# A decoder layer on one core: the weight sums of the MLP's product 5 in the tiles of product 7, and two tiles in place of three for the down projection's operands

## The chip, the cores and the metric

The kernel runs on one NeuronCore of one Trainium2 chip. The metric is the device time of one execution in microseconds (us); the kernel before took 1101.72 us, the median of 3 runs (1101.19 to 1101.97).

## What is computed

The reference is one decoder layer on 512 tokens of width 1024, in float32: a retention branch and a latent attention branch, an output projection, an MLP and a gated embedding. The change touches only the MLP, which comes near the end:

```python
h2 = rms_norm(x, norm_mlp)
x = x + jnp.square(jax.nn.relu(h2 @ w_up)) @ w_down     # w_up 1024x4096, w_down 4096x1024
gate = jax.nn.sigmoid(rms_norm(x, norm_ple) @ w_ple_gate)
x = x + gate * (p_l @ w_ple)
```

## The kernel before

All matrix products are made with float32r operands that are split in two: a high part (ScalarE, ACT in the profile, by a copy) and a low part (VectorE, DVE, by a subtraction), and three matmuls in place of one (`mm3`). Weights pass through the same split: `load_chunk` (line 247) makes `wh_...` on ACT and then `wl_...` on DVE from a raw tile of 128x1024 floats, 512 KB.

The MLP's hidden width of 4096 is worked in four groups (`gg` 0 to 3). The up product of group 0 is a plain product of eight chunks (`up`, line 973; chunks `wr_up_0_0` to `wr_up_0_7`, here "up chunk 0" to "up chunk 7"). All other products, the up products of groups 1 to 3 (`up_seven`, line 1024, called u1 to u7) and the down products of all groups (`down`, line 1084, called dn1 to dn7), are made by a scheme with seven half-size products in place of eight, in the order 1, 7, 2, 6, 5, 4, 3. Each product needs two weight chunks (`c` 0 and 1), which are quarters of the weight or sums of them:

- products 1, 2 and 3 use a quarter as it is: one load by the SyncE queue (SP);
- product 7 is loaded by SP and then gets a second quarter added by a DMA that accumulates, which GpSimd (POOL) issues; products 6 and 4 add one more quarter each to the same tile, so that this tile lives from product 7 to product 4;
- product 5 is loaded by SP and gets one quarter added by a DMA of POOL.

`prepare` (line 218) issues these. Raw tiles come from two sets: `wraw`, six tiles in the pool `wpool`, named `wr_...`, for everything that is loaded as it is and, in the MLP, also for product 5; and `draw`, four tiles in the pool `tw` that is opened for the tail, named `dr_...`, for product 7. SP issues its loads in order; a load into a tile waits until the DVE has made the low part of the chunk that was there before. The tile framework's scheduler sets the order of instructions on each engine from the tiles that are free, so a number of tiles changes the order.

A line of code (1365) sets how down and up products alternate: `"1 v3 7 u1 2 6 u7 5 4 u6 3 u2 u5 u4"`, where a number is a down product of this group, `u` an up product of the next group and `v3` product 3 of this group's up. The last group runs `"1 v3 7 2 e 6 e 5 4 3"`, where `e` is part of a small other product. The down product's left operand is split by `xsplit` (line 1050) into `ch` and `cl` tiles, 4 KB per partition each; three of each rotate. `combine` (line 1055) makes the operand of the next down product just ahead of the present one.

Before the seven-product scheme can start, the normalised input is read back from DRAM: `up_norm` (line 989) loads `x2n` in two halves of 1 MB (line 992, DMAs on SP) and scales it in eight DVE instructions (line 994); `up_operand` (line 996) makes the operands `xu...` from it. The prediction speaks of the two halves' landing as T0 and T1. `up_out` (line 978) evacuates the plain up product (`f`, lines 984 and 985).

Of the kernel before, what the change touches and what calls it, by code (L numbers as in the profile page):

```python
# [31 lines left out]
F32R = mybir.dt.float32r  # L32
# [19 lines left out]

C_ID, C_MASK, C_IND, C_INVR, C_INVM, C_SGN, C_N = 0, 128, 256, 260, 261, 262, 263

NDYN, NKEEP, NW, NRAW, NDRAW, AHEAD, PREP, EARLY, PAD = 45, 16, 3, 6, 4, 1, 3, 5, 104
GROUPS = DFF // 1024


# [90 lines left out]
def trunk_layer(ctx: ExitStack, tc: tile.TileContext, xT, pT, pos, gains, const, decay, wstream, outT):  # L149
# [61 lines left out]
    def chunk(key):  # L211
        width, o = spec[key][0], offset[key]
        fetched.add(key)
        return wstream[o:o + P * width].rearrange("(p c) -> p c", p=P)
# [3 lines left out]
    def prepare(key):  # L218

        if key[0] == "sw":  # L220
            _, blk, p, c = key

            def more(raw, kb, fb):
                nc.gpsimd.dma_start(raw, chunk(("w", blk, kb, fb, c)), accum_op=ALU.add)  # L224

            if p in (6, 4):
                return more(dw[blk, "t", c], *((0, 0) if p == 6 else (1, 0)))
            kb, fb = {1: (0, 0), 7: (0, 1), 2: (1, 0), 5: (0, 1), 3: (1, 1)}[p]
            nm = f"{blk[0]}{blk[1]}{p}{c}"
            if p == 7 and blk[0] in ("dn", "up"):  # L230
                raw = tail_pool["w"].tile([P, 1024], F32, tag="draw", name="dr_" + nm, bufs=NDRAW)
            else:
                raw = wpool.tile([P, 1024], F32, tag="wraw", name="wr_" + nm, bufs=NRAW)
            nc.sync.dma_start(raw, chunk(("w", blk, kb, fb, c)))
            dw[blk, "t" if p == 7 else p, c] = raw
            if p == 7:
                more(raw, 1, 1)
            elif p == 5:
                more(raw, 0, 0)
            return  # L240
        width = spec[key][0]
        nm = "_".join(str(x) for x in key)
        raw = wpool.tile([P, width], F32, tag="wraw", name="wr_" + nm, padded_shape=[P, 1024], bufs=NRAW)
        tc.keep_in_program_order(nc.sync.dma_start(raw, chunk(key))) if key[0] == "a1" else nc.sync.dma_start(raw, chunk(key))
        dw[key] = raw
# [25 lines left out]
    def run_steps():  # L271
        order = list(dict.fromkeys(k for k, _, _ in steps if k is not None))
        rank = {k: i for i, k in enumerate(order)}
        loaded, prepared = len(wt), len(dw)
        for key, fn, args in steps:
            if key is not None:
                while loaded < min(len(order), rank[key] + 1 + AHEAD):
                    if prepared == loaded:
                        prepare(order[prepared])
                        prepared += 1  # L280
                    load_chunk(order[loaded])
                    loaded += 1
                while prepared < min(len(order), rank[key] + 1 + PREP) and (tail_pool or order[prepared][0] == "sw"):
                    prepare(order[prepared])
                    prepared += 1
                fn(wt[key], *args)
            else:
                fn(*args)
        assert fetched == set(spec), fetched ^ set(spec)
# [12 lines left out]
    def split(src, name, scale=None, hi=None, lo=None, pin=False):  # L302

        hi = T(name + "h", F32R) if hi is None else hi
        lo = T(name + "l", F32R) if lo is None else lo
        if scale is None:
            ACT(hi, src, AF.Copy)
            TT(lo, src, hi.bitcast(F32), op=ALU.subtract)  # L308
        else:
            i = ACT(hi, src, AF.Copy, scale=scale)  # L310
            if pin:
                tc.keep_in_program_order(i)
            STT(lo, src, scale, hi.bitcast(F32), op0=ALU.mult, op1=ALU.subtract)  # L313
        return hi, lo
# [52 lines left out]
    for k in range(8):  # L367
        xs.append(T(f"x{k}"))
        if k < 6:
            prepare(("a1", k))  # L370
        tc.keep_in_program_order(nc.sync.dma_start(xs[k], xT[:, k]))
# [584 lines left out]
    def A(name, shape, tag, bufs, dtype=F32):  # L956
        return tail_pool["a"].tile([P, *shape], dtype, tag=tag, name=name, bufs=bufs)
# [90 lines left out]
            STT(t, t, 0.0, t, op0=ALU.max, op1=ALU.mult)  # L1048

    def xsplit(gg, p, src, scale=None):  # L1050
        hi = A(f"ch{gg}{p}", (4, 256), "ch", 3, F32R)
        lo = A(f"cl{gg}{p}", (4, 256), "cl", 3, F32R)
        X[gg, p] = split(src, None, scale, hi=hi, lo=lo)

    def combine(gg, p):

        f1, f2 = F[gg, 0], F[gg, 1]
        a11, a21, a12, a22 = f1[:, :, 0:256], f1[:, :, 256:512], f2[:, :, 0:256], f2[:, :, 256:512]

        def tmp(nm):  # L1060
            return A(f"{nm}_{gg}", (4, 256), "cs", 2)

        if p == 1:
            xsplit(gg, p, a11, -1.0)
        elif p == 7:
            X["s"] = tmp("s")
            TT(X["s"], a21, a11, op=ALU.subtract)  # L1067
            xsplit(gg, p, X["s"])
        elif p in (6, 3):
            TT(X["s"], a22 if p == 6 else a12, X["s"], op=ALU.subtract)  # L1070
            xsplit(gg, p, X["s"])
        elif p == 2:
            xsplit(gg, p, a12)
        elif p == 5:
            t = tmp("s1")
            TT(t, a21, a22, op=ALU.subtract)
            xsplit(gg, p, t)
        else:
            xsplit(gg, p, a22, -1.0)
# [142 lines left out]
    for h in range(MH):  # L1222
        p, more = h // 2, h + 2 < MH
# [144 lines left out]
    for gg in range(GROUPS):  # L1368
        last, quarter = gg + 1 == GROUPS, 0
        for s_ in "1 v3 7 2 e 6 e 5 4 3".split() if last else seq:  # L1370
# [5 lines left out]
            elif s_[0] in "uv":  # L1376
                g_, p = gg + (s_[0] == "u"), int(s_[1])
# [4 lines left out]
            else:  # L1382
                p = int(s_)
# [74 lines left out]
```

## Time and profile before

| | |
|---|---|
| median of 3 runs | 1101.72 us (1101.19 to 1101.97) |
| the profiled execution | 1101.0 us, its span 1099.2 us |
| PE busy | 1085.2 us, 99% of the span |
| DVE busy | 757.9 us, 69% |
| ACT busy | 565.8 us, 51% |
| POOL busy | 111.1 us, 10% |
| moved by DMA | 195.91 MB |
| plain queue q1 (issued by SP) | 134.90 MB, 35.7% of the 16 DMA engines' time |
| accumulating queue q0 (issued by POOL) | 60.04 MB, 27.3% |

PE is TensorE's matmul row. Times in the views count from the start of the span. In a timeline a row has the start, the duration, the engine, the line, the operation, the tile written and the tiles read; what stands in brackets is the idle time of that engine just before and what ended it. SPq and POOL rows of DMAs are issues, not transfers. The MLP runs from about 711 us (first up chunk) to about 1040 us.

### The profile page before, as it was taken

What the parts mean: (1) busy time and instruction counts of PE and PEld (TensorE: products, weight loads), DVE (VectorE), ACT (ScalarE), POOL (GpSimd) and SP (SyncE); (2) the same over time, 40 slices, a digit from 0 to 9 for tenths busy, and PEclk for the clock granted to TensorE, in tenths of its full rate; (3) what the DMA queues carried; (4) which work ended last, traced back from release to release, by engine and by line L of the source; (5) the groups of instructions that cost most, each with busy time, mean ns of one, the idle gap of its engine ahead of it and who ended that gap; (6) DMA issues with size and microseconds to landing.
All of it is one profiled execution on the core that took longest, in us unless ns stands there. A gap on an engine that the chain in (4) does not pass through costs nothing. (4 is left out here: it accounts for less than half of the span.)

```text
span 1099.2 us, 14887 instructions
## 1 busy us (share of the span) xinstructions
PE 1085.2 (99%) x5569; PEld 923.3 (84%) x5569; DVE 757.9 (69%) x1176; ACT 565.8 (51%) x817; POOL 111.1 (10%) x145
## 2 busy tenths in 40 slices
PE   9999999999999999999999999999999999999998
PEld 7778888888888888888888888887899899898887
DVE  7697677566774655655465467649869769769784
ACT  7647656444466545344554644426645545546541
POOL 0000000000112001122100100011111111201000
PEclk9999999999999999999999999999999999999999
DMA  7232231356778744498864934694998999979511
GB/s 261 71 120 87 72 107 50 133 199 212 206 190 241 193 157 159 121 196 213 204 205 118 286 126 148 199 305 117 229 267 222 229 272 220 238 217 279 154 47 58
DMA packets 64616, 195.91 MB, mean 178 GB/s; under 512 B 7904, under 2 KB 9312, under 8 KB 64160
## 3 DMA queue, kind: packets, MB, share of 16 engines
q1 hardware_dynamic: 46464, 134.90, 35.7%
q0 software_dynamic: 17936, 60.04, 27.3%
q8 instruction: 44, 0.72, 0.3%
q14 instruction: 28, 0.23, 0.1%
q10 hardware_dynamic: 144, 0.03, 0.0%
HBM read 175.80 MB, written 17.04 MB: 175 GB/s over the span
## 5 line engine op out<-in xcount | busy, mean ns | idle before, releaser
L169 PE MATMUL dn<-wl_dn,ch 128*128 128x512 f32 x224 | 87.7, 391 | 1.5 <-DVE wl_dn L266 1.5
L169 PE MATMUL dn<-wh_dn,cl 128*128 128x512 f32 x224 | 87.7, 391 | 1.4 <-DVE cl L308 0.9
L169 PE MATMUL dn<-wh_dn,ch 128*128 128x512 f32 x224 | 87.2, 389 | 0.0
L262 ACT ACTIVATE wh_up<-wr_up 128x1024 fp32r<-128x1024 f32 x32 | 33.9, 1058 | 44.1 <-PE us L169 13.4
L266 DVE TENSOR_TENSOR wl_up<-wr_up,wh_up 128x1024 fp32r<-128x1024 f32 x32 | 39.1, 1221 | 24.4 <-ACT wh_up L262 24.0
L262 ACT ACTIVATE wh_dn<-wr_dn 128x1024 fp32r<-128x1024 f32 x32 | 33.9, 1059 | 34.1 <-PE us L169 16.5
L169 PEld LDWEIGHTS dn<-wh_dn,cl 128*128 128x128 f32 x224 | 42.1, 188 | 10.5 <-DVE cl L308 1.3
L169 PEld LDWEIGHTS dn<-wl_dn,ch 128*128 128x128 f32 x224 | 42.1, 188 | 10.3 <-DVE wl_dn L266 2.3
L169 PEld LDWEIGHTS dn<-wh_dn,ch 128*128 128x128 f32 x224 | 42.1, 188 | 8.8
L266 DVE TENSOR_TENSOR wl_dn<-wr_dn,wh_dn 128x1024 fp32r<-128x1024 f32 x32 | 39.0, 1220 | 10.7 <-ACT wh_dn L262 10.6
L262 ACT ACTIVATE wh_rv<-wr_rv 128x1024 fp32r<-128x1024 f32 x28 | 29.7, 1059 | 30.6 <-issue 9.9
L262 ACT ACTIVATE wh_rg<-wr_rg 128x1024 fp32r<-128x1024 f32 x28 | 29.6, 1059 | 30.4 <-PE rg L169 12.1
L266 DVE TENSOR_TENSOR wl_rg<-wr_rg,wh_rg 128x1024 fp32r<-128x1024 f32 x20 | 24.5, 1226 | 23.5 <-ACT wh_rg L262 23.4
L224 POOL DMA_DIRECT2D dr_dn<-wstream x24 | 21.9, 957 | 173.2 <-DVE rx L331 95.9
L266 DVE TENSOR_TENSOR wl_dn<-dr_dn,wh_dn 128x1024 fp32r<-128x1024 f32 x24 | 29.3, 1220 | 13.9 <-ACT wh_dn L262 13.9
L266 DVE TENSOR_TENSOR wl_rv<-wr_rv,wh_rv 128x1024 fp32r<-128x1024 f32 x20 | 24.4, 1223 | 16.2 <-ACT wh_rv L262 16.2
L266 DVE TENSOR_TENSOR wl_br<-wr_br,wh_br 128x1024 fp32r<-128x1024 f32 x16 | 19.5, 1221 | 19.7 <-ACT wh_br L262 19.7
L1105 DVE TENSOR_TENSOR d<-d,dn 128x1024 f32<-128x1024 f32 x24 | 29.2, 1217 | 5.4 <-PE dn L169 5.4
L262 ACT ACTIVATE wh_up<-dr_up 128x1024 fp32r<-128x1024 f32 x18 | 19.1, 1062 | 25.9 <-PE dn L169 14.1
L262 ACT ACTIVATE wh_dn<-dr_dn 128x1024 fp32r<-128x1024 f32 x24 | 25.3, 1053 | 13.1 <-PE dn L169 6.5
L262 ACT ACTIVATE wh_br<-wr_br 128x1024 fp32r<-128x1024 f32 x16 | 16.9, 1058 | 21.0 <-issue 12.8
L873 ACT ACTIVATE rt<-br 128x512 f32<-128x512 f32 x24 | 13.9, 594 | 25.8 <-PE br L169 25.8
(1889 smaller groups left out, 3690.2 us busy)
## 6 DMA issues: line engine op xcount, KB each, us to landing
wr_up<-wstream SPq DMA_DIRECT2D x32, 512.0 KB, 5.6
wr_dn<-wstream SPq DMA_DIRECT2D x32, 512.0 KB, 6.9
dr_dn<-wstream POOLq DMA_DIRECT2D x24, 512.0 KB, 9.5
wr_rv<-wstream SPq DMA_DIRECT2D x20, 512.0 KB, 4.1
wr_rg<-wstream SPq DMA_DIRECT2D x20, 512.0 KB, 5.0
dr_up<-wstream POOLq DMA_DIRECT2D x18, 512.0 KB, 9.0
wr_rv<-wstream POOLq DMA_DIRECT2D x16, 512.0 KB, 6.5
wr_rg<-wstream POOLq DMA_DIRECT2D x16, 512.0 KB, 6.9
```

Source lines behind the costliest of these rows:

```text
L169: return tc.keep_in_program_order(nc.tensor.matmul(*a, **k))
L224: nc.gpsimd.dma_start(raw, chunk(("w", blk, kb, fb, c)), accum_op=ALU.add)
L262: i = ACT(hi, raw, AF.Copy, scale=sign)
L266: TT(lo, raw, hi.bitcast(F32), op=ALU.subtract)
L873: ACT(t, ps, AF.Copy)
L1105: TT(to, to, dps[p], op=ALU.add if sign > 0 else ALU.subtract)
```

## The change

```diff
-NDYN, NKEEP, NW, NRAW, NDRAW, AHEAD, PREP, EARLY, PAD = 45, 16, 3, 6, 4, 1, 3, 5, 104
+NDYN, NKEEP, NW, NRAW, NDRAW, AHEAD, PREP, EARLY, PAD = 45, 16, 3, 6, 6, 1, 3, 5, 104
...
-            if p == 7 and blk[0] in ("dn", "up"):
+            if p in (7, 5) and blk[0] in ("dn", "up"):
                 raw = tail_pool["w"].tile([P, 1024], F32, tag="draw", name="dr_" + nm, bufs=NDRAW)
             else:
                 raw = wpool.tile([P, 1024], F32, tag="wraw", name="wr_" + nm, bufs=NRAW)
...
     def xsplit(gg, p, src, scale=None):
-        hi = A(f"ch{gg}{p}", (4, 256), "ch", 3, F32R)
-        lo = A(f"cl{gg}{p}", (4, 256), "cl", 3, F32R)
+        hi = A(f"ch{gg}{p}", (4, 256), "ch", 2, F32R)
+        lo = A(f"cl{gg}{p}", (4, 256), "cl", 2, F32R)
         X[gg, p] = split(src, None, scale, hi=hi, lo=lo)
```

In the MLP the two raw tiles of product 5 come from `draw`, which grows from four to six tiles; `wraw` keeps six tiles, which now serve plain loads alone. The operands `ch` and `cl` have two tiles each in place of three. The memory is the same (two tiles of 4 KB per partition come, two go). No computation changes, PE's instructions stand in the same order, and the number of instructions is the same on every engine. The order on SP, DVE and ACT changes.

On SP, at the first down products. Names: `dr_up_7135` is the load of u7's second chunk, 7154 and 7174 are the two chunks of dn5 of group 0, `x2n` the two halves of the input read back.

```order
 L234 DMA wr_dn_6849<-wstream 128x1024
 L234 DMA dr_up_7135<-wstream 128x1024
+L234 DMA dr_dn_7154<-wstream 128x1024
+L234 DMA dr_dn_7174<-wstream 128x1024
 L992 DMA x2n_6698<-x2d 128x2048
 L992 DMA x2n_6768<-x2d 128x2048
```

The two loads for dn5 stand ahead of the two halves of `x2n`. Before, they stood behind them, after the loads for u1 and dn2:

```order
 L234 DMA wr_dn_6995<-wstream 128x1024
 L234 DMA wr_dn_7014<-wstream 128x1024
-L234 DMA wr_dn_7154<-wstream 128x1024
-L234 DMA wr_dn_7174<-wstream 128x1024
 L234 DMA wr_dn_7305<-wstream 128x1024
 L234 DMA wr_dn_7332<-wstream 128x1024
```

On POOL the accumulating DMAs of group 0 keep their places (two for dn7, two for u7, two for dn5, then dn6's); those of dn5 write `dr_dn` tiles in place of `wr_dn`, and no longer have to wait until dn1's weights have left those tiles.

On the DVE, at the same place. `x2n_6698` and `x2n_6768` are the two halves, `wl_up_6` is the weight of up chunk 6, `xu1l` the low part of u1's operand, `f` the evacuation of an up product, `cl_6918` the operand of dn1.

```order
 L266 TENSOR_TENSOR wl_up_5_6775<-wr_up_5_6708,wh_up_5_6774 128x1024
 L994 SCALAR_TENSOR_TENSOR x2n_6698<-x2n_6698,gn,bcx_6692 128x512 x4
-L994 SCALAR_TENSOR_TENSOR x2n_6768<-x2n_6768,gn,bcx_6692 128x512
+L313 SCALAR_TENSOR_TENSOR xu1l<-x2n_6698,xu1h 128x512
 L984 SCALAR_TENSOR_TENSOR f_6694<-up_6710,bcx_6692 128x512 x2
-L994 SCALAR_TENSOR_TENSOR x2n_6768<-x2n_6768,gn,bcx_6692 128x512 x3
+L994 SCALAR_TENSOR_TENSOR x2n_6768<-x2n_6768,gn,bcx_6692 128x512 x4
 L266 TENSOR_TENSOR wl_up_6_6806<-wr_up_6_6739,wh_up_6_6805 128x1024
-L313 SCALAR_TENSOR_TENSOR xu1l<-x2n_6698,xu1h 128x512 x2
+L313 SCALAR_TENSOR_TENSOR xu1l<-x2n_6698,xu1h 128x512
 L313 SCALAR_TENSOR_TENSOR cl_6918<-f_6694,ch_6917 128x1024
 L266 TENSOR_TENSOR wl_up_7_6846<-wr_up_7_6778,wh_up_7_6845 128x1024
```

One `xu1l` and the two `f` now stand between the two halves of `x2n`; before, one instruction of the second half stood ahead of the two `f`. From `wl_up_7` on the order is the same up to dn7's second weight, `wl_dn_6973`. From there to u1's weights, `wl_up_6992` and `wl_up_7011`:

```order
 L1070 TENSOR_TENSOR s_6921<-f_6835,s_6921 128x1024
 L266 TENSOR_TENSOR wl_dn_6973<-dr_dn_6931,wh_dn_6972 128x1024
+L1076 TENSOR_TENSOR s_0_7125<-f_6694,f_6835 128x1024
+L313 SCALAR_TENSOR_TENSOR xu4l_7430<-x2n_6768,xu4h_7428 128x512
 L308 TENSOR_TENSOR cl_6969<-f_6835,ch_6968 128x1024
-L1076 TENSOR_TENSOR s_0_7125<-f_6694,f_6835 128x1024
 L266 TENSOR_TENSOR wl_up_6992<-wr_up_6951,wh_up_6991 128x1024
+L266 TENSOR_TENSOR wl_up_7011<-wr_up_6976,wh_up_7010 128x1024
```

The half-size `xu4l` has moved ahead of u1's first weight, and the work that stood between u1's two weights has moved behind them.

On the DVE in group 1, as in groups 2 and 3, at dn2, dn6 and u7 (`wl_dn_7853` is dn2's second weight, 7871 and 7897 are dn6's, `wl_up_7916` is u7's first, `cl_7893` the operand of dn5, `d_6965` the evacuation of dn2):

```order
 L266 TENSOR_TENSOR wl_dn_7853<-wr_dn_7788,wh_dn_7852 128x1024
-L308 TENSOR_TENSOR cl_7893<-s_1_7890,ch_7892 128x1024
 L1070 TENSOR_TENSOR s_7634<-f_7071,s_7634 128x1024
 L266 TENSOR_TENSOR wl_dn_7871<-dr_dn_7663,wh_dn_7870 128x1024
 L266 TENSOR_TENSOR wl_dn_7897<-dr_dn_7683,wh_dn_7896 128x1024
 L1105 TENSOR_TENSOR d_6965<-d_6965,dn_7857 128x2x512
+L308 TENSOR_TENSOR cl_7893<-s_1_7890,ch_7892 128x1024
 L266 TENSOR_TENSOR wl_up_7916<-dr_up_7874,wh_up_7915 128x1024
```

The operand of dn5 is made after dn2 has been evacuated, ahead of u7's weight; its high part on ACT stands at the same place. Its tile is the one that dn2 read.

## Prediction

> **What bounds the kernel now.** I read the page's busy table first, then where PE waits, then the DVE around those waits, then the DMA queues ahead of them.
>
> ```profile
> span 1099.2 us, 14887 instructions
> PE 1085.2 (99%) x5569; PEld 923.3 (84%) x5569; DVE 757.9 (69%) x1176; ACT 565.8 (51%) x817; POOL 111.1 (10%) x145
> ```
>
> PE is busy for 99%; the change leaves its instructions and their order alone, so only PE's waits can move. PE's timeline shows four in the MLP:
>
> ```profile
> 761.87 0.51 PE L169 MATMUL dn<-wh_dn,cl 128*128 128x512 f32 x1 [0.54 <-ACT wh_dn L262]
> 763.88 0.50 PE L169 MATMUL dn<-wl_dn,ch 128*128 128x512 f32 x1 [1.50 <-DVE wl_dn L266]
> 770.16 0.39 PE L169 MATMUL us<-xu1h,wl_up 128*128 128x256 f32 x1 [0.62 <-DVE wl_up L266]
> 1006.79 0.50 PE L169 MATMUL dn<-wh_dn,cl 128*128 128x512 f32 x1 [0.87 <-DVE cl L308]
> ```
>
> Three, 0.54 + 1.50 + 0.62 = 2.66 us, lie at dn7 and the start of u1; with the 0.87 us of the last group, 3.53 us is all that could be won here. The table of windows by tens shows why: the DVE is full there, PE is not.
>
> ```profile
> 740.00:750.00 10.00, 10.00 (x46) 8.28 (x45) 10.00 (x13) 4.38 (x6) 0.00 (x0) 1.00 0.45 152
> 750.00:760.00 10.00, 10.00 (x45) 8.15 (x44) 10.00 (x13) 7.26 (x11) 0.87 (x1) 1.00 0.29 75
> 760.00:770.00 10.00, 7.50 (x30) 5.10 (x28) 10.00 (x12) 8.95 (x11) 2.62 (x3) 1.00 0.72 162
> ```
>
> The columns are the window's length, then PE, PEld, DVE, ACT, POOL busy, clock, DMA share, GB/s. The DVE's full stretch begins where its timeline shows the last long wait:
>
> ```profile
> 733.93 2.74 DVE L994 SCALAR_TENSOR_TENSOR x2n<-x2n,gn,bcx 128x512 f32<-128x512 f32 x4 [2.93 <-DMA x2n<-x2d]
> 738.99 0.75 DVE L994 SCALAR_TENSOR_TENSOR x2n<-x2n,gn,bcx 128x512 f32<-128x512 f32 x1 [2.32 <-DMA x2n<-x2d]
> 739.66 1.28 DVE L984 SCALAR_TENSOR_TENSOR f<-up,bcx 128x512 f32<-128x512 f32 x2
> 740.86 2.07 DVE L994 SCALAR_TENSOR_TENSOR x2n<-x2n,gn,bcx 128x512 f32<-128x512 f32 x3
> 742.84 1.22 DVE L266 TENSOR_TENSOR wl_up<-wr_up,wh_up 128x1024 fp32r<-128x1024 f32 x1
> 743.98 1.28 DVE L313 SCALAR_TENSOR_TENSOR xu1l<-x2n,xu1h 128x512 fp32r<-128x512 f32 x2
> ```
>
> So T0 is 733.93 and T1 738.99: from T1 on the DVE works without a gap to u1's weight, which PE awaits at 770.16. What sets the time of this place is when `x2n` lands and how much DVE work follows. It lands late because the DMA engines are full:
>
> ```profile
> 720.00:728.00 8.00, 8.00 (x39) 6.60 (x38) 2.82 (x6) 2.61 (x3) 1.64 (x2) 1.00 1.02 251
> 728.00:739.00 11.00, 11.00 (x50) 9.13 (x49) 3.97 (x6) 3.28 (x4) 0.86 (x1) 1.00 1.04 307
> ```
>
> (DMA share 1.02 and 1.04.) The issues on SP and POOL:
>
> ```profile
> 719.44 0.33 SPq L234 DMA_DIRECT2D wr_dn<-wstream  x1
> 719.81 0.43 SPq L234 DMA_DIRECT2D dr_up<-wstream  x1
> 720.35 1.23 SPq L992 DMA_DIRECT2D x2n<-x2d  x2
> ```
>
> ```profile
> 721.12 0.87 POOL L224 DMA_DIRECT2D dr_up<-wstream  x1 [0.35 <-issue]
> 729.50 0.86 POOL L224 DMA_DIRECT2D dr_up<-wstream  x1 [7.51 <-DMA dr_up<-wstream]
> 757.40 0.87 POOL L224 DMA_DIRECT2D wr_dn<-wstream  x1 [27.04 <-DVE xu6l L308]
> 764.51 0.86 POOL L224 DMA_DIRECT2D wr_dn<-wstream  x1 [6.25 <-DVE xu6l L308]
> ```
>
> `x2n` is issued at 720.35 and needs till 733.93 and 738.99, behind dn1's and u7's loads on its own queue and beside u7's accumulations on the other. The last two rows are dn5's accumulations, now some 37 us behind `x2n`'s issue.
>
> **The change part by part.**
>
> *Two loads move ahead of `x2n`.* In the new SP order dn5's two loads, 2 x 512 KB, stand between u7's second load and `x2n`. Their tiles are free, so they go out at about 720.3, and `x2n` about 0.8 us later (two issues of 0.33 to 0.43 us), which costs nothing while the queue is backed up. What they cost `x2n` is their transfer time. The queue's own rows for two stretches:
>
> ```profile
> q0 software_dynamic: 173, 0.64, 55.5%
> q1 hardware_dynamic: 286, 1.08, 48.0%
> ```
>
> (722 to 728: plain 4 KB packets on q1, dn1's and u7's loads, beside accumulations on q0; packets, MB, share of the engines' time.)
>
> ```profile
> q0 software_dynamic: 321, 1.18, 53.9%
> q1 hardware_dynamic: 322, 2.20, 49.9%
> ```
>
> (728 to 739: `x2n` on q1 beside u7's accumulations on q0.)
>
> Lower bound: q1 alone. 286 packets took 48.0% of 16 x 6 us, 0.161 us each; 256 packets over 16 engines take 2.6 us. Upper bound: packet by packet with q0, as in 728 to 739 (322 against 321). A q0 packet took 55.5% of 96 us / 173 = 0.308 us; 16 pairs of 0.469 us per engine are 7.5 us. Between them lies the nearest row: the same kind of loads beside the same accumulations moved 1.08 MB in 6 us, so 1.05 MB takes 5.8 us. I take 5.8, because q0 stays backed up in the new order too: after u7's second accumulation (POOL at 729.50) come dn5's two, some 25 us earlier than now (they wait for their loads, which land from about 732 on), one before `x2n`'s first half has landed. T0 becomes 739.7 and T1 744.8.
>
> The Trainium skill ("DMA: Bandwidth & Descriptors", section "Queues, rings and completion order") says that each DMA engine goes round the queues with work, one packet each. The 728 to 739 rows agree, those of 722 to 728 don't (173 to 286: q0 ran dry between two accumulations); by the rule alone the shift would be the upper 7.5 us.
>
> *DVE work leaves the stretch behind T1.* Two `f` (739.66 to 740.86, 1.20 us) and one `xu1l` (half of 743.98 to 745.18, 0.60 us) now stand between T0 and T1. T0 + 2.7 (four `x2n`) + 0.6 + 1.2 = T0 + 4.5, and T1 follows T0 by 5.1, so they fit into the wait: -1.8 us. If the halves landed closer together, up to 0.6 us of it would come back.
>
> *One `xu4l` enters it,* ahead of u1's first weight:
>
> ```profile
> 773.43 0.68 DVE L313 SCALAR_TENSOR_TENSOR xu4l<-x2n,xu4h 128x512 fp32r<-128x512 f32 x1
> 774.04 1.21 DVE L266 TENSOR_TENSOR wl_dn<-wr_dn,wh_dn 128x1024 fp32r<-128x1024 f32 x1
> ```
>
> 774.04 - 773.43 = 0.6 us: +0.6. The rest between T1 and u1 is the same work.
>
> *Sum.* u1 starts at 770.16 + 5.8 - 1.8 + 0.6 = 774.8: +4.6 us. PE's other limit there is earlier. Up chunk 6 needs its `wl_up`, now made right after four `x2n`: T1 + 2.65 + 1.22 = 748.7, while PE wants it at
>
> ```profile
> 744.75 0.39 PE L169 MATMUL up<-x2g0h,wl_up 128*128 128x512 f32 x1
> ```
>
> so PE stops there for 3.9 us, a wait that is not in the profile now. From there PE needs 770.16 - 744.75 - 2.66 = 22.75 us of work to u1, to 771.5; the DVE is later, at 774.8. Behind u1 the DVE has caught up by its next gap, 2.40 us long:
>
> ```profile
> 789.12 1.23 DVE L266 TENSOR_TENSOR wl_dn<-wr_dn,wh_dn 128x1024 fp32r<-128x1024 f32 x1 [2.40 <-ACT wh_dn L262]
> ```
>
> *dn5's accumulations leave 757 to 772.* POOL's waits of 27.04 and 6.25 us go; nothing waits for POOL there: 0. dn6's additions behind them can only come earlier: 0.
>
> *Two `ch`/`cl` tiles.* Where two down products adjoin (2-6, 5-4; in the last group 7-2 and 5-4), the operand after next can only be made once PE has left the earlier one. In group 1, dn2 ends where dn6 starts, and u7 must be ready 5.5 us later:
>
> ```profile
> 854.67 10.91 PE dn L169 x48
> 865.58 5.75 PE us L169 x48
> ```
>
> ```profile
> 860.18 1.22 DVE L1105 TENSOR_TENSOR d<-d,dn 128x1024 f32<-128x1024 f32 x1 [0.40 <-PE dn L169]
> 861.32 1.22 DVE L266 TENSOR_TENSOR wl_up<-dr_up,wh_up 128x1024 fp32r<-128x1024 f32 x1
> ```
>
> The DVE's evacuation starts at 860.18; the operand goes in behind it for 1.14 us, and u7's weight ends at 863.7 in place of 862.5, 1.9 us before PE wants it. ACT's part, one more copy of about 1 us, fits as well: it waits for PE there.
>
> ```profile
> 860.18 1.06 ACT L262 ACTIVATE wh_up<-dr_up 128x1024 fp32r<-128x1024 f32 x1 [1.66 <-PE dn L169]
> ```
>
> Covered: 0. Without that cover each such place costs what it is late.
>
> *Other groups.* More raw tiles let loads go earlier; PE waits for none there now: 0. The 0.87 us at 1006 waits for dn2's operand, whose place is unchanged: 0.
>
> The profiled execution took 1101.0 us (span 1099.2 and 1.8 around it): 1101.0 + 4.6 = 1105.6. The median of the runs is 0.7 above it, so 1106.3.
>
> **The rivals.**
>
> *Mostly alone on the queue.* If q0 runs dry while dn5's loads pass, the shift is near 2.6: 2.6 - 1.2 = +1.4, 1103.1. For it: 173 against 286 packets. Against: more accumulations are queued than then.
>
> *No delay.* If `x2n` is held by something other than bytes ahead, only the DVE's gain is left: -1.2, 1100.5. Against: full DMA engines.
>
> *Earlier is better (faster).* dn5's loads and sums are issued some 25 us earlier and no longer share 757 to 772 with the stretch in which PE waits. If DMA traffic is what makes weights late there, all 3.53 us go: 1098.2. It decides if T1 stays at 739.0 or before; each us later takes one back. Against: the three waits end on ACT and DVE, the DVE is full at a DMA share of 0.29 too. The Trainium skill ("DMA: Bandwidth & Descriptors", section "Rules for kernel authors") advises to issue a DMA early and to wait for it late; no row here shows a gain from that.
>
> *Two tiles cost.* If u7's weight (or its like) ends more than 1.9 us later than worked out, each of the 8 adjoining places costs; 0.5 us each is 4 us on top: 1110.3. Against: the 1.9 us, and ACT's idle 1.66 us.
>
> **How the numbers follow.** Forecast (shift 3.4 to 7.5, +2.2 to +6.3): 0.68. Mostly alone: 0.14. No delay: 0.06. Earlier is better: 0.05. Two tiles cost: 0.07. A measurement of this kernel tells 0.2%, 2.2 us, from no change. Slower: 0.68 + 0.07 = 0.75; within: 0.14 + 0.06 = 0.20; faster 0.05. The range goes from +1.4 less half a us (the runs lie within 0.8) to +6.3 and half a us: 1102.6 to 1108.5, leaving out 0.18.
>
> **What would show it.** Right: `x2n`'s issues behind two `dr_dn`, its two landings near 739.7 and 744.8; a PE wait of about 4 us at up chunk 6; u1 starting near 775; dn5's accumulations on POOL before 745; no new PE wait behind u1. Wrong: T1 within 2 us of 739 (the shift), u1's delay far from T1's less 1.2 (the DVE sum), or PE waits for `cl` or `wl` behind 786 (the two tiles).

## The result and the profile after

The changed kernel takes 1107.3 us (median of 6 runs, 1106.16 to 1108.47) beside 1101.85 us before (median of 6, taken with it): a ratio of 1.0051, 95% interval 1.0040 to 1.0062, so 5.45 us more. The profiled execution took 1108.47 us, the longest of the six, with a span of 1106.7. One execution of the kernel before (1347.8 us) and one of the changed kernel with dn5's loads behind `x2n` (1820.2 us, at a granted clock of 0.56) were slow throughout, and no ratio or trace below goes by them.

The page's busy table:

```profile
span 1106.7 us, 14887 instructions
PE 1088.9 (98%) x5569; PEld 926.5 (84%) x5569; DVE 758.2 (69%) x1176; ACT 565.5 (51%) x817; POOL 110.8 (10%) x145
```

Instructions and busy times are those of before, except that PE shows 3.7 us more: matmuls that ran at a lower clock, below. SP's timeline at the first down products, and POOL's:

```profile
719.24 0.33 SPq L234 DMA_DIRECT2D wr_dn<-wstream  x1
719.61 0.43 SPq L234 DMA_DIRECT2D dr_up<-wstream  x1
720.09 1.12 SPq L234 DMA_DIRECT2D dr_dn<-wstream  x2
721.27 1.39 SPq L992 DMA_DIRECT2D x2n<-x2d  x2
```

```profile
730.44 0.86 POOL L224 DMA_DIRECT2D dr_up<-wstream  x1 [7.79 <-DMA dr_up<-wstream]
734.23 0.86 POOL L224 DMA_DIRECT2D dr_dn<-wstream  x1 [2.94 <-DMA dr_dn<-wstream]
735.30 0.86 POOL L224 DMA_DIRECT2D dr_dn<-wstream  x1 [0.21 <-issue]
```

The two loads of dn5 stand ahead of `x2n`, whose issue is 0.92 us later (720.35 before); dn5's sums are issued at 734 and 735, before `x2n` has landed. On the DVE its two halves now begin at

```profile
739.81 2.74 DVE L994 SCALAR_TENSOR_TENSOR x2n<-x2n,gn,bcx 128x512 f32<-128x512 f32 x4 [9.02 <-DMA x2n<-x2d]
...
745.10 2.74 DVE L994 SCALAR_TENSOR_TENSOR x2n<-x2n,gn,bcx 128x512 f32<-128x512 f32 x4 [0.75 <-DMA x2n<-x2d]
747.75 1.21 DVE L266 TENSOR_TENSOR wl_up<-wr_up,wh_up 128x1024 fp32r<-128x1024 f32 x1
```

so T0 is 5.88 and T1 6.11 us later. PE's waits in the MLP, from its timeline:

```profile
749.12 0.77 PE L169 MATMUL up<-x2g0h,wl_up 128*128 128x512 f32 x1 [4.41 <-DVE wl_up L266]
775.07 0.39 PE L169 MATMUL us<-xu1h,wl_up 128*128 128x256 f32 x1 [1.20 <-DVE wl_up L266]
1012.63 0.50 PE L169 MATMUL dn<-wh_dn,cl 128*128 128x512 f32 x1 [1.80 <-DVE cl L308]
```

The first is the new stop at up chunk 6. The two waits at dn7 (0.54 and 1.50) are gone, since PE comes there later. u1 starts at 775.07, 4.91 us later than before. The third row is in the last group: 1.80 us where it was 0.87. The windows by tens (PE's clock is the third figure from the end) beside those shown of before:

```profile
740.00:750.00 10.00, 5.59 (x23) 4.38 (x22) 9.25 (x14) 5.28 (x6) 0.00 (x0) 0.86 0.97 282
750.00:760.00 10.00, 10.00 (x37) 8.01 (x37) 10.00 (x12) 4.26 (x6) 0.00 (x0) 0.80 0.45 145
760.00:770.00 10.00, 10.00 (x45) 7.95 (x44) 10.00 (x14) 9.10 (x14) 0.86 (x1) 1.00 0.19 64
```

From 750 to 760 PE starts 37 matmuls in place of 45, at a granted clock of 0.80. Nothing in the prediction reckoned with that.

This execution's span is 7.5 us longer: 4.91 at u1, 1.80 - 0.87 = 0.93 at the last group (1012.63 against 1006.79 is 5.84 = 4.91 + 0.93), and 1.66 behind it.

### The profile page after: what moved, and what is told of

The parts are those of the page before. It is cut to its first block, busy times and chain, and to the rows that moved or that the text cites. A ratio compares the mean times of both kernels' runs of the same rounds, so it can differ in the third digit from the quotient of the medians.

```text
span 1106.7 us, 14887 instructions
## 1 busy us (share of the span) xinstructions
PE 1088.9 (98%) x5569; PEld 926.5 (84%) x5569; DVE 758.2 (69%) x1176; ACT 565.5 (51%) x817; POOL 110.8 (10%) x145
## 4 chain that ended last, share of the span: by engine, by line
PE 87%; DVE 6%; DMA 3%; issue 2%; ACT 2%; SPq 0%; DVEq 0%; ACTq 0%
PE dn L169 12%; PE us L169 10%; PE br L169 8%; PE rv L169 7%; PE rg L169 7%; PE pg L169 4%; PE gr L169 4%; PE rk L169 4%; PE bm L169 4%; PE rq L169 4%; PE wo L169 4%; PE gm L169 3%; PE ro L169 2%; DMA x2n<-x2d 2%; PE sc L169 2%
## 5 line engine op out<-in xcount | busy, mean ns | idle before, releaser
L224 POOL DMA_DIRECT2D dr_dn<-wstream x32 | 27.6, 864 | 274.0 <-DVE wl_dn L266 133.9
L266 DVE TENSOR_TENSOR wl_dn<-dr_dn,wh_dn 128x1024 fp32r<-128x1024 f32 x32 | 39.1, 1222 | 23.2 <-ACT wh_dn L262 23.0
L262 ACT ACTIVATE wh_up<-wr_up 128x1024 fp32r<-128x1024 f32 x26 | 27.4, 1059 | 36.3 <-issue 13.0
L266 DVE TENSOR_TENSOR wl_up<-wr_up,wh_up 128x1024 fp32r<-128x1024 f32 x26 | 31.7, 1221 | 18.1 <-ACT wh_up L262 17.8
L262 ACT ACTIVATE wh_dn<-dr_dn 128x1024 fp32r<-128x1024 f32 x32 | 33.7, 1054 | 19.7 <-PE dn L169 14.7
L262 ACT ACTIVATE wh_up<-dr_up 128x1024 fp32r<-128x1024 f32 x24 | 25.4, 1057 | 23.0 <-PE us L169 15.5
L262 ACT ACTIVATE wh_dn<-wr_dn 128x1024 fp32r<-128x1024 f32 x24 | 25.4, 1057 | 22.7 <-PE us L169 13.0
L266 DVE TENSOR_TENSOR wl_up<-dr_up,wh_up 128x1024 fp32r<-128x1024 f32 x24 | 29.3, 1222 | 9.7 <-ACT wh_up L262 9.7
L266 DVE TENSOR_TENSOR wl_dn<-wr_dn,wh_dn 128x1024 fp32r<-128x1024 f32 x24 | 29.2, 1218 | 5.3 <-ACT wh_dn L262 5.1
L224 POOL DMA_DIRECT2D dr_up<-wstream x24 | 21.8, 998 | 79.6 <-DMA dr_up<-wstream 32.1
```

The lines of the kernel that those rows point to most:

```text
L262: i = ACT(hi, raw, AF.Copy, scale=sign)
L266: TT(lo, raw, hi.bitcast(F32), op=ALU.subtract)
```

## The experiments

The theory was the prediction's: the bytes of dn5 ahead of `x2n` delay it, the DVE is full from T1 on, and u1 follows T1 at a fixed distance. The rivals: the two `ch`/`cl` tiles or the DVE's new order cost the time, or `x2n` is held by something else. In what follows T1 is the start of the DVE's work on the second half, read from the rows; where the DVE waits for that half, this is its landing.

**dn5's loads behind `x2n`.** An order without a wait, from `x2n`'s second load to every MLP load of the seven-product scheme but those that stood ahead of it before:

```diff
-        nc.sync.dma_start(t, x2d[:, 4 * j:4 * j + 4])
+        V["x2n"] = nc.sync.dma_start(t, x2d[:, 4 * j:4 * j + 4])
...
-            nc.sync.dma_start(raw, chunk(("w", blk, kb, fb, c)))
+            i = nc.sync.dma_start(raw, chunk(("w", blk, kb, fb, c))); LATE and tc.add_manual_dep(i.ins, V["x2n"].ins.name, NOSYNC, reason="order")
```

(LATE: a `dn` or `up` block, and not product 1 or 7 of dn group 0 or up group 1. NOSYNC: an edge that sets the order of issue alone.)

> The changed kernel with one order restored: the two loads of dn5 of group 0 are issued behind the two halves of x2n (and behind u1's two loads); the new tiles and the two ch/cl tiles stay. The theory (these 2 x 512 KB ahead of x2n are the loss at u1): the x2n scalings of the DVE start at 733.9 and 739.0 again, no stop of PE at up chunk 6, u1 at 770.2 + 0.6 = 770.8. The wait at the last group stays at 1.8 us in place of 0.87. Total 1101.85 + 0.6 + 0.9 = 1103.4, up to 1.7 more if the clock is halved after that wait: 1103.4 to 1105.1. Rival (the tiles or the DVE's order behind x2n make the loss): u1 stays near 775 and the total at 1107.

Measured: 1102.7 us (before 1101.83 beside it), ratio 1.0006, interval 0.9997 to 1.0015. The loss is gone but for a part that can't be told from none. The time is below the 1103.4 to 1105.1 expected: that sum took the last group's 1.80 us for a fixed part of the change, and in the trace below this wait is 0.88 us. The same kernel once more, for its trace:

> The kernel with dn5's two loads behind x2n once more, for its profile. The theory: the x2n scalings start within 1 us of 733.9 and 739.0, no wait of PE at up chunk 6, PE waits at dn7 and u1 as before, u1 at 770.8 (0.6 later than before, the xu4l that stands ahead of its weight), and a clock of 1.00 from 740 to 770. Rival (the rest of the change adds to the delay): u1 later than 772.

Its rows on the DVE and PE:

```profile
735.62 2.74 DVE L994 SCALAR_TENSOR_TENSOR x2n<-x2n,gn,bcx 128x512 f32<-128x512 f32 x4 [4.46 <-DMA x2n<-x2d]
740.13 0.75 DVE L994 SCALAR_TENSOR_TENSOR x2n<-x2n,gn,bcx 128x512 f32<-128x512 f32 x1 [1.78 <-DMA x2n<-x2d]
```

```profile
745.35 0.47 PE L169 MATMUL up<-x2g0h,wl_up 128*128 128x512 f32 x1 [0.28 <-DVE wl_up L266]
...
771.91 0.38 PE L169 MATMUL us<-xu1h,wl_up 128*128 128x256 f32 x1 [1.22 <-DVE wl_up L266]
```

T0 and T1 are 1.7 and 1.1 us later than in the profile of before, a little beyond the 1 us expected, with `x2n` issued at the same time (720.44 against 720.35). Two executions of the changed kernel differ by 1.0 and 1.5 us (below), so this can be chance; it isn't shown to be. u1 is T1 + 31.78, where it was 31.17 before: the 0.6 us for the `xu4l`.

**The two tiles alone.** The kernel before with `ch` and `cl` at two tiles:

```diff
-        hi = A(f"ch{gg}{p}", (4, 256), "ch", 3, F32R)
-        lo = A(f"cl{gg}{p}", (4, 256), "cl", 3, F32R)
+        hi = A(f"ch{gg}{p}", (4, 256), "ch", 2, F32R)
+        lo = A(f"cl{gg}{p}", (4, 256), "cl", 2, F32R)
```

> The kernel before with ch and cl at two tiles each; product 5 stays among the plain loads. The theory (two tiles are covered): 1101.85, within 1 us, the wait for cl in the last group at 0.87 us, u1 0.6 us later at most. Rival (two tiles cost where two down products adjoin): up to 8 x 0.5 = 4 us more, 1105.9, with PE waits for cl or wl behind u1. Second rival (the longer wait in the last group comes from the two tiles): that wait is 1.8 us here too, and the total 1102.8 to 1104.5.

Measured: 1102.18 us, ratio 1.0006 (0.9997 to 1.0015). Its T1 and u1:

```profile
739.50 0.75 DVE L994 SCALAR_TENSOR_TENSOR x2n<-x2n,gn,bcx 128x512 f32<-128x512 f32 x1 [2.28 <-DMA x2n<-x2d]
```

```profile
771.28 0.39 PE L169 MATMUL us<-xu1h,wl_up 128*128 128x256 f32 x1 [1.22 <-DVE wl_up L266]
```

Again 31.78 us apart. So the 0.6 us come from the two tiles, which move the `xu4l` ahead of u1's weight; nothing else that they cost can be told. The wait in the last group is 0.88 us here, and PE has no wait between u1 and that place: the rival of up to 4 us falls.

**One load ahead.** In the first edit, LATE also spares chunk 0 of dn5 of group 0.

> The changed kernel with only the first of dn5's two loads ahead of x2n; the second is issued behind x2n and u1's loads. The DVE's order is that of before at the two halves of x2n. If the shift goes with the bytes ahead (5.8 us for 1 MB with its sums): 2.9 us, T0 736.8, T1 741.9, u1 = 770.16 + 2.9 + 0.6 = 773.7, total 1101.8 + 3.5 = 1105.3. If a load alone on its queue sets it (2.6 us for 1 MB): 1.3 us, u1 at 772.1, total 1103.7. If two loads are needed for a delay (x2n is held by something else): no shift, 1102.5.

Measured: 1105.91 us, ratio 1.0037 (1.0024 to 1.0049; before 1102.28 beside it), against the 1105.3 for a shift that goes with the bytes.

```profile
738.38 2.74 DVE L994 SCALAR_TENSOR_TENSOR x2n<-x2n,gn,bcx 128x512 f32<-128x512 f32 x4 [6.94 <-DMA x2n<-x2d]
743.45 0.75 DVE L994 SCALAR_TENSOR_TENSOR x2n<-x2n,gn,bcx 128x512 f32<-128x512 f32 x1 [2.34 <-DMA x2n<-x2d]
```

```profile
775.23 0.38 PE L169 MATMUL us<-xu1h,wl_up 128*128 128x256 f32 x1 [1.22 <-DVE wl_up L266]
```

One load of 512 KB shifts T1 by 3.9 us from the mean of the three executions with the old place (738.99, 739.50, 740.13: 739.54), somewhat more than half of the 6.4 us that two do. In this trace T1 and u1 are 1.5 us later than a shift by bytes was expected to make them. u1 is T1 + 31.78 once more.

**The loads without their sums.**

```diff
-            elif p == 5:
+            elif p == 5 and blk != ("dn", 0):
                 more(raw, 0, 0)
```

> The changed kernel without the two accumulating transfers into dn5's weights of group 0 (this sum is left out, so product 5 of that group uses one of its two blocks alone); the plain loads stay ahead of x2n. It tells how much of the 5.8 us belongs to the sums that run beside x2n from 734.2 on. If they take half the engines' turns from then to 739.8: T0 up to 2.4 us earlier (737.4), T1 earlier by 2 to 4 us (741 to 743), total 1107.3 - 2 to - 4 = 1103.3 to 1105.3. Rival (the loads alone make the shift): T0 739.8, T1 745, 1107.3.

Measured: 1105.0 us, ratio 1.0026 (1.0016 to 1.0037), beside 1106.65 for the changed kernel in the same series.

```profile
739.77 2.74 DVE L994 SCALAR_TENSOR_TENSOR x2n<-x2n,gn,bcx 128x512 f32<-128x512 f32 x4 [8.62 <-DMA x2n<-x2d]
744.23 2.73 DVE L994 SCALAR_TENSOR_TENSOR x2n<-x2n,gn,bcx 128x512 f32<-128x512 f32 x4
```

T1 is 1.7 us earlier than the mean of the three executions with both loads and sums ahead (745.10, 746.60, 746.11: 745.94), and the total 1.65 us lower; T1 was expected 2 to 4 us earlier, at 741 to 743. The row of the second half has no wait here: the DVE comes to it straight from its other work, after the half has landed. The view of line 992 gives the landing:

```profile
L992 SPq DMA_DIRECT2D x2n<-x2d x2: 471/578/684, 721.7 to 722.5; - x2
DMA to landing us min/median/max: 18.1/19.6/21.1
```

The second half lands 21.1 us after its issue at 722.5, at 743.6. So the sums hold its landing up by about 2.3 us, of which the DVE feels 1.7. T0 is 0.7 us earlier: for most of the first half the sums come too late. What they take shows in the DMA view from 734 to 740 (packets, MB, share), without the sums and then with them (the changed kernel again, below):

```profile
q1 hardware_dynamic: 225, 1.50, 61.4%
q0 software_dynamic: 138, 0.50, 41.7%
```

```profile
q0 software_dynamic: 179, 0.67, 55.7%
q1 hardware_dynamic: 184, 1.20, 50.1%
```

With dn5's sums q0 takes 41 packets more and q1, on which `x2n` comes, 41 fewer (in the first profile of the changed kernel 157 and 202: 19 more and 23 fewer).

**The changed kernel again.** The wait of 1.80 us in the last group stood against the prediction's 0.87, so a second profile was taken.

> The changed kernel once more, unaltered, for a second profile. Open is whether the longer wait in the last group (1.80 us for cl in place of 0.87) and the half clock after it belong to the change or to that one execution. If they belong to the change (praw's load always 6.7 us): 1.8 us again. If not: 0.9 us, a span of 1104 to 1105.5. In both cases the stop at up chunk 6 is 4 to 5.5 us, the clock is near half for a few us behind it, and u1 starts at 774.5 to 776.5.

Measured: 1106.65 us, ratio 1.0043 (1.0028 to 1.0058). PE's waits and T1:

```profile
750.62 0.76 PE L169 MATMUL up<-x2g0h,wl_up 128*128 128x512 f32 x1 [5.83 <-DVE wl_up L266]
776.57 0.38 PE L169 MATMUL us<-xu1h,wl_up 128*128 128x256 f32 x1 [1.22 <-DVE wl_up L266]
...
1013.50 0.50 PE L169 MATMUL dn<-wh_dn,cl 128*128 128x512 f32 x1 [1.17 <-DVE cl L308]
```

```profile
746.60 2.74 DVE L994 SCALAR_TENSOR_TENSOR x2n<-x2n,gn,bcx 128x512 f32<-128x512 f32 x4 [1.22 <-DMA x2n<-x2d]
```

The stop at chunk 6 is there again (5.83 us, a little over the 4 to 5.5 expected), u1 is T1 + 29.97 as in the first profile (745.10 and 775.07), and the last group's wait is 1.17 us, between the 0.9 and the 1.8 expected. In the first profile ACT and the DVE show how 1.80 came about:

```profile
1003.64 1.06 ACT L307 ACTIVATE pph<-praw 128x1024 fp32r<-128x1024 f32 x1 [2.66 <-DMA praw<-pT]
```

```profile
1005.68 1.23 DVE L266 TENSOR_TENSOR wl_dn<-dr_dn,wh_dn 128x1024 fp32r<-128x1024 f32 x1 [1.07 <-ACT wh_dn L262]
```

ACT stands 2.66 us for `praw`, the DVE stands 1.07 us for the weight half queued behind it on ACT, and PE gets its operand that much later. ACT's same wait is 2.03 us in this second execution; it is 1.69 in the trace with dn5 behind `x2n`, and there PE's wait is 0.88: up to about 1.7 us it is covered.

**`praw` out of the last group's queue.**

```diff
-        t = A("praw", (2, S), "cs", 2)
+        t = A("praw", (2, S), "xs", 5)
```

> The changed kernel with the tile praw (loaded from pT) among the xs tiles in place of the cs tiles, so that its load, and with it the reload of x's last two tiles, is issued well ahead of the last group. The theory (in the last group ACT stands 2.66 us for praw, whose load takes 6.7 us in place of 4.5, and everything behind is late by 1.07): the wait for cl falls from 1.80 us to 0.7 or less and PE's clock stays at 1.00 there; u1 stays near 775. Total 1107.3 - 1.1 to - 3.5 = 1103.8 to 1106.2. Rival (the DVE's own work or the two tiles make that wait): it stays at 1.8 us and the total at 1107.

Measured: 1107.26 us, ratio 1.0051 (1.0038 to 1.0063). PE's wait in the last group is 0.88 us and its clock 1.00 there, as the theory had it, but no gain can be told in the median: expected was 1.1 to 3.5 us less than 1107.3. `x2n` landed late in the profiled execution (T1 746.11, u1 776.09, again 29.98 apart). So the 2.6 us of the last group (0.93 + 1.66) are seen in the first profiled execution and are not a fixed cost of the change; how many of the runs without a trace have them isn't known. Why `praw` takes 4.5 us in one trace and 6.7 in another stays open; other loads stand behind it now, but with the same loads around it it also took 5.2, 5.4 and 6.0.

**`x2n` first.** LATE is now every `dn` and `up` block, so the two halves go out ahead of all MLP loads of weight sums.

> The changed kernel with the two halves of x2n issued ahead of all MLP weight sums' loads (dn1, dn7, u7, dn5). The theory (x2n's landing sets u1): x2n lands before 725, the DVE's two waits for it (2.93 and 2.32 us before) go, PE's waits at dn7 and u1 (2.66 us) go with them, u1 at 770.16 - 2.66 = 767.5. Total 1101.85 - 2.66 + 0.9 = 1100.1, up to 1.7 more by the clock after the last group's wait: 1100.1 to 1101.8. Rival: dn1's and dn7's loads and sums, now behind 2 MB, come late in their turn: PE waits at dn1 or dn7, 1103 or more.

> The changed kernel with x2n first once more, beside the kernel before with x2n first on the same chip. Same as then: 1096.9 within 0.7 us; u1 at 766.1.

Measured: 1096.93 us, ratio 0.9956 (0.9943 to 0.9968), and 1097.1 the second time. `x2n` is issued at 711.59 in place of 721.27; the DVE no longer waits for it, and PE has no wait at all from 700 to the last group:

```profile
730.47 3.40 DVE L994 SCALAR_TENSOR_TENSOR x2n<-x2n,gn,bcx 128x512 f32<-128x512 f32 x5
```

```profile
744.31 0.39 PE L169 MATMUL up<-x2g0h,wl_up 128*128 128x512 f32 x1
...
766.07 0.28 PE L169 MATMUL us<-xu1h,wl_up 128*128 128x256 f32 x1
```

That is over 3 us better than the 1100.1 to 1101.8 expected: 0.9 of it because the last group's wait was 0.88 and not 1.80, 1.0 because PE loses more by its waits than their rows say (below); the rest is spread (chunk 6 starts 0.44 us earlier already, and before's median lies 0.7 above its profile). From chunk 6 to u1 PE takes 766.07 - 744.31 = 21.76 us here and took 770.16 - 744.75 = 25.41 before: 3.65 us, where the rows of the waits added up to 2.66.

**The kernel before with `x2n` first.** The same edit on the kernel before, product 5 still among the plain loads and three `ch`/`cl` tiles; only SP's order differs from before.

> The kernel before (product 5 among the plain loads, three ch/cl tiles) with the two halves of x2n issued ahead of all MLP loads of weight sums; nothing else moves on any engine. If x2n's landing is all that matters and the change's tiles bring nothing by themselves: PE has no wait from 700 to 1000, u1 at 766 to 767, total within 1 us of the changed kernel with x2n first, 1096.9 to 1098. Rival (the tiles of the change bring part of that kernel's gain): 1099 or more, with a PE wait left at dn7, u1 or dn5.

Measured: 1097.2 us, ratio 0.9956 (0.9943 to 0.9970); no wait of PE from 700 to the last group, u1 at

```profile
766.85 0.28 PE L169 MATMUL us<-xu1h,wl_up 128*128 128x256 f32 x1
```

Beside 1097.1 with the change on the same chip: once `x2n` is out of the way, the tiles of the change neither cost nor bring anything that can be told. Both kernels beat the two that this study began with.

## Why the prediction was right

T0, T1 and u1 in the eight traces in which `x2n` is issued behind the loads of dn1, dn7 and u7 (in the last row the DVE waits for the first half alone, and T1 is where it starts on the second):

| kernel | T0 | T1 | u1 | u1 - T1 |
|---|---|---|---|---|
| before | 733.93 | 738.99 | 770.16 | 31.17 |
| two tiles alone | 734.48 | 739.50 | 771.28 | 31.78 |
| dn5 behind `x2n` | 735.62 | 740.13 | 771.91 | 31.78 |
| one load ahead | 738.38 | 743.45 | 775.23 | 31.78 |
| changed | 739.81 | 745.10 | 775.07 | 29.97 |
| changed again | 740.84 | 746.60 | 776.57 | 29.97 |
| `praw` early | 740.80 | 746.11 | 776.09 | 29.98 |
| no sums for dn5 | 739.77 | 744.23 | 774.19 | 29.96 |

- *The DVE's sum* (T1 less 1.8 and plus 0.6) was exact: 31.17 + 0.61 = 31.78 with the `xu4l` alone, and 29.97 where the two `f` and one `xu1l` stand between the halves as well. T1 decides, whatever delays it, as long as the DVE waits there. That an `xu4l` moves ahead was put down to the change as a whole; it comes from the two tiles.
- *The shift* was taken at 5.8 us between 2.6 and 7.5. T0 moved by 5.8 (means of three executions, 740.48 against 734.68), T1 by 6.4 (745.94 against 739.54). The nearest row was the right guide, and this term was 0.6 us too small at the half that counts. By the DVE's sum u1 is then 6.4 - 1.2 = 5.2 us later, where 4.6 was forecast. That is most of the 0.85 between the 4.6 and the 5.45 measured. Of the 6.4 us at the second half's landing the two sums have about 2.3, in the one trace without them, and the loads about 4.1. This is more than the 2.6 of loads alone on their queue, so they do pass beside other work. By the round-robin rule of the Trainium skill ("DMA: Bandwidth & Descriptors", section "Queues, rings and completion order") it would have been 7.5, by the prediction's estimate; the mean here doesn't reach that, a single pair of traces (746.60, 7.6 after 738.99) does.
- *PE's stop at up chunk 6* was forecast at 3.9 us and was 4.41, 5.51 and 5.83: the same step, longer by T1's lateness.
- *No cost in the other groups* held: no trace has a PE wait between u1 and the last group. *The last group's wait "unchanged"* was wrong in the profiled execution (1.80 us, and 1.66 by the clock behind it), half right in the second (1.17), and right in the other five traces of the changed last group (0.88).
- *"3.53 us is all that could be won here"* failed: 4.6 us were won by moving `x2n` alone, though the 0.87 us of the last group stayed (0.88). The step added up the idle times of PE's rows up to u1, 2.66 us, and those leave out about a quarter of the 3.65 that PE loses there. It also reckoned from one execution of before that lay 0.8 us below the median of its kernel: the spans of the two profiled executions differ by 3.3 us (1099.2 and 1095.9).
- *The rivals.* No delay and mostly alone on the queue fall by T1; earlier is better falls, since dn5's sums at their new place bring nothing even where `x2n` is early (1097.1 against 1097.2); two tiles cost falls by the run with them alone.

## What to carry to other kernels

A free tile lets a load go out early, and a load with time to spare then stands ahead of one that is late already (here dn5's weights were issued at 720.09, and ACT took the first of them at 792.95): when buffers are added, look at what the queue now sends ahead of the transfer that the next stage waits for. Where an engine is full from a landing on, the time behind that landing is a fixed sum of its work and could here be worked out from the order to a tenth of a us; the uncertain term is the landing. Moving the awaited load itself to the front was worth more here than either arrangement of the buffers.

## What the runs showed of the hardware

**PE's granted clock fell after a wait of under 2 us.** Behind the stop at up chunk 6 and behind the 1.80 us in the last group the granted clock is lower for a few us. PE's timeline at the latter:

```profile
1009.99 0.39 PE L169 MATMUL dn<-wh_dn,cl 128*128 128x512 f32 x1
1010.22 0.39 PE L169 MATMUL dn<-wl_dn,ch 128*128 128x512 f32 x1
...
1013.49 0.63 PE L169 MATMUL dn<-wh_dn,cl 128*128 128x512 f32 x1
1013.91 0.63 PE L169 MATMUL dn<-wl_dn,ch 128*128 128x512 f32 x1
1014.34 0.63 PE L169 MATMUL dn<-wh_dn,ch 128*128 128x512 f32 x1
```

A matmul starts every 0.23 us ahead of the wait and every 0.42 behind it. The window with that stretch in the first profile, and the same stretch in the second, where the wait was 1.17 us:

```profile
1012.50:1015.80 3.30, 3.17 (x9) 2.50 (x10) 3.30 (x4) 0.42 (x1) 0.00 (x0) 0.63 0.72 274
```

```profile
1012.30:1015.70 3.40, 2.23 (x10) 1.80 (x10) 3.40 (x5) 2.01 (x2) 0.00 (x0) 1.00 1.00 294
```

In these traces waits of 1.80, 3.17, 3.32, 4.41, 5.51 and 5.83 us were followed by it and none of 1.58 or less was. At up chunk 6 it costs nothing, because the DVE is later still (u1 keeps a wait of 1.2 us); in the last group, where PE is the bound, it costs the 1.66 us: the nine steps from 1013.20 to 1016.85 alone take 1.58 us more than nine of 0.23. The Trainium skill ("TensorE: Matmul & The Clock Gate", section "What's actually happening") has the half clock set in after an idle window of about 3.4 us; here 1.80 us of idle were enough once.

**A wait row understates the loss.** At u1 before, the row says 0.62 us, but the start of the matmul ahead of it is

```profile
769.15 0.39 PE L169 MATMUL dn<-wh_dn,ch 128*128 128x512 f32 x1
770.16 0.39 PE L169 MATMUL us<-xu1h,wl_up 128*128 128x256 f32 x1 [0.62 <-DVE wl_up L266]
```

1.01 us earlier, where the step without a wait is 0.23: 0.78 lost. The idle time counts from a matmul's modelled end (0.39 us) and not from when the next could have started. The two waits at dn7 lose 0.16 and 0.28 us more than their rows say in the same way, and three steps of 0.29 to 0.34 us ahead of u1 are too short to get a wait of their own.

**A load's landing differs by over 1 us between executions of one kernel.** In two executions of the changed kernel T1 is 745.10 and 746.60, with `x2n` issued at 721.27 and 721.55. In the three kernels with `x2n` in the old place, one execution each, it is 738.99, 739.50 and 740.13.
